# mLSTM scalings, decay and normalising moved to ScalarE; the last block's keys in a free operand's buffer; RWKV's first dense products issued beside that block

## The chip, the cores and the metric

The kernel runs on one core of one Trainium2 chip. The metric is the time of one execution on the device, in microseconds (us), as the median of several runs. The engines are named as in the profile: PE is TensorE's matrix multiply and PEld its weight load, DVE is VectorE, ACT is ScalarE, POOL is GpSimd, and SP is SyncE, whose queue issues all DMAs here.

## The reference, cut to what matters

One layer with four groups of heads (RWKV-7, pooling, mLSTM, retention) over 4096 tokens of 1024 channels: one input projection, four mixers of 256 channels each, one output projection with a gated embedding and a layer norm. The change concerns the mLSTM mixer and the first block of RWKV:

```
def mlstm_mix(qk, v, ig_pre, fg_pre, o_pre, conv_w, i_bias, f_bias, ln_w):
    qk = silu(causal_dwconv(qk, conv_w))          # 4 taps
    q, k = split(qk)
    ...
    d_log = where(causal, b[..., :, None] - b[..., None, :] + log_i[..., None, :], -inf)
    ...
    scores = einsum('bhcld,bhcsd->bhcls', q, k) * exp(d_log - m_t[..., None])
    num = einsum('bhcls,bhcsv->bhclv', scores, v) + s_inter * einsum('bhcvk,bhclk->bhclv', c_prev, q)
    den = sum(scores, -1) + s_inter * einsum('bhck,bhclk->bhcl', n_prev, q)
    h = num / maximum(abs(den), exp(-m_t))
    h = h * sigmoid(o_pre)
    h = head_norm(h) * ln_w

def rwkv7_mix(z, mu, ...):
    prev = pad(z)[:, :-1]
    z = z + (prev - z) * mu
    r, k, v, wl, al = split(z)
    ...
```

The mLSTM output is then multiplied by `silu(ml_g)`.

## The kernel before, in words

The tokens are worked in 16 blocks of 256 (`TB`), stage after stage: pooling, retention, mLSTM, RWKV (with the output gate's embedding), output. A dense product splits each operand into a rounded high part and a rest (`fetch`, L84 and L85: ACT casts, DVE or POOL subtracts) and adds three products into PSUM. The raw tiles of that split rotate through three buffers.

In `_mlstm`, `dense(b)` makes block b's projections: queries and keys as `zqk` (L145 to L147), and values, gates and output gates by seven products of Strassen's kind (`zoa` to `zod`, L1375 to L1377), whose operands lie in the weight pool and in the pool `mq`. `mix(b)` does the rest for the block: the convolution of queries and keys into `xc` (L1187 to L1194, tanh on ACT), then for each of two chunks of 128 tokens the decay `D` (a subtract and a maximum against the mask `big` on DVE, L1206; the exponential on ACT, L1209), scores `scm` (L1214), masked scores (L1216), `num` (L1219), the inter-chunk part `it` (L1222), the keys turned and scaled, `kt` and `kw` (L1227, L1229), the state update `dsm` and `Sm` (L1234, L1238), the sum `tot` (L1243, L1244) and the quotient (L1247 to L1251); then the gate, `head_norm` (L722 to L730; a power on POOL, L727), the weight `lnw` on POOL (L1255), the second gate (L1256) and the store. The loop calls `dense(i)` and `mix(i - 1)`, and a scheduler that follows its own estimates merges them into one fixed order on each engine. `xc` has one buffer (`XC`), `D` too (`DB`).

RWKV runs as a table of stages (`ORDER`), of which for block 0 the first are `la` (the low-rank columns), `k` and `r`: each is a dense product over eight pairs of input channels (`zla0`, 24 products; `z0k` and `z0r`, 48 each) and a mix with the token before (`mixed`, L264 to L268). The stage `l` takes `la` through the small matrices `LW` (loaded as `lraw`, split at L219 and L220), and `n` makes the key norms from squares `sq` on ACT (L366). `lraw`, a zeroed buffer that is written out to DRAM (L245 to L251) and `sq` share one buffer, in that order.

Of the kernel before, what the change touches and what calls it, by code (L numbers as in the profile page):

```python
# [42 lines left out]
class Trunk:  # L43
# [148 lines left out]
    def _rwkv_out(self, es):  # L192
# [16 lines left out]
        wg = [self.lazy("w_rw", i * G) for i in range(3)]  # L209
        wla = self.lazy("w_rw", 3 * G, P)  # L210
        wgate = self.lazy("w_rw", 3 * G + P)
        prm, omu = self.prm, self.omu
# [44 lines left out]
        def mixed(b, out, z, c0, n):  # L257

            zf, zl = bl[b]["zf"], bl[b]["zl"]
            with self.soon():  # L260
                A.copy(out=zl[:, c0:c0 + n], in_=z[:, :, TB - 1:TB].rearrange("p a o -> p (a o)"))
                for p in range(n):
                    c = c0 + p
                    A.mul(out=out[:, p], in_=z[:, p], mul=omu[:, c:c + 1])  # L264
                    V.scalar_tensor_tensor(out=out[:, p, 1:], in0=z[:, p, 0:TB - 1], scalar=prm[:, c:c + 1],
                                           in1=out[:, p, 1:], op0=ALU.mult, op1=ALU.add)
                first = out[:, :, 0:1].rearrange("p a o -> p (a o)")
                V.tensor_tensor(out=first, in0=first, in1=zf[:, c0:c0 + n], op=ALU.add)  # L268
# [25 lines left out]
        @stage  # L294
        def la(b):
            if b == 0:
                for w in (wla, wg[1], wg[0], wg[2]):
                    w()
            x = self.load_x(b)
            zf = self.zp.tile([P, 7], F32, name=f"zf{b}", tag="zf", bufs=2)  # L300
            zl = self.zp.tile([P, 7], F32, name=f"zl{b}", tag="zl", bufs=2)
            if b == 0:
                Q.memset(zf, 0.0)
            else:
                Q.tensor_tensor(out=zf, in0=bl[b - 1]["zl"], in1=prm[:, 0:7], op=ALU.mult)
            bl[b] = dict(zf=zf, zl=zl, x=x)
# [4 lines left out]
            la_ = self.zp.tile([P, 1, TB], F32, name=f"la{b}", tag="la", bufs=1)  # L311
            mixed(b, la_, z, 6, 1)
            la = la_[:, 0]
            with self.soon():
                A.activation(out=la[0:64], in_=la[0:64], func=AF.Tanh)
            bl[b]["la"] = la
# [1373 lines left out]
```

## Time and profile before

| | |
|---|---|
| median of 3 runs | 2850.34 us (2846.73 to 2855.72) |
| the profiled execution | 2850.36 us |
| its span, first to last instruction | 2848.6 us |
| PE / DVE / POOL / ACT busy | 95% / 80% / 40% / 34% |
| mean granted TensorE clock | 0.974 |
| mLSTM in the span | from about 656 us to 1260 us |

The profile is that of one execution. Busy shares are averages over stages with different limits; the granted clock is the share of TensorE's full 2.4 GHz that it was given, 0.50 being the lower of the two levels, 1.2 GHz. Idle time of an engine is shown with what ended it, and the chain of waits follows the work that ended last. Times in the traces are microseconds from the span's start.

### The profile page before, as it was taken

The numbers are of one execution on the slowest core, as the hardware profiler recorded it, in microseconds if no ns is written. First come the engines' busy times: TensorE is split into PE (matmuls) and PEld (weight loads), VectorE is DVE, ScalarE is ACT, GpSimd is POOL, SyncE is SP. The second block draws the span as 40 slices with busy tenths as digits, with TensorE's granted clock in tenths as the row PEclk, the third lists the DMA queues.
The fourth block names the chain that finished last, engine by engine and source line by source line (L and its number), as shares of the span: only waits on it lengthen the run. The fifth ranks groups of instructions, "written<-read, shape, count | busy, mean of one in ns | idle before, by whom it ended". The sixth has DMA issues, their size and how long they took to land.

```text
span 2848.6 us, 57425 instructions
## 1 busy us (share of the span) xinstructions
PE 2703.9 (95%) x21940; PEld 2422.4 (85%) x21940; DVE 2266.1 (80%) x5639; ACT 971.6 (34%) x2100; POOL 1142.9 (40%) x1263
## 2 busy tenths in 40 slices
PE   7799999998999999968999999999998999899997
PEld 7798888887999999958999999998887888777885
DVE  5767888887999999986888888888655666689997
ACT  3423232234433333323443434334322333432221
POOL 6555555554333333330232333224225111256665
PEclk9999999999999999969999999999999999999998
DMA  7753221223311111221111111113347444643441
GB/s 237 220 153 102 64 65 58 60 67 102 97 55 56 53 53 57 81 81 45 38 49 39 48 42 46 44 43 86 118 148 242 143 137 137 219 151 140 154 150 67
DMA packets 250500, 281.13 MB, mean 99 GB/s; under 512 B 69488, under 2 KB 166512, under 8 KB 250224
## 3 DMA queue, kind: packets, MB, share of 16 engines
q1 hardware_dynamic: 250224, 277.46, 31.0%
q8 instruction: 172, 2.82, 0.4%
q14 instruction: 104, 0.85, 0.1%
HBM read 209.69 MB, written 67.70 MB: 97 GB/s over the span
## 4 chain that ended last, share of the span: by engine, by line
PE 32%; DVE 14%; DMA 4%; POOL 3%; issue 3%; ACT 1%; SPq 0%; POOLq 0%; DVEq 0%; ACTq 0%
PE ry L273 3%; DVE ro L1582 2%; DVE ro L1561 1%; PE sa L273 1%; DVE ro L1564 1%; PE zg L154 1%; POOL ro L1565 1%; PE zg L155 1%; PE zg L156 1%; DVE so L1556 1%; PE zpe L145 1%; PE ds L273 1%; PE zpe L147 1%; DVE g L463 1%; PE zpe L146 1%
## 5 line engine op out<-in xcount | busy, mean ns | idle before, releaser
L1340 ACT CAST Ah<-xr 128x512 fp32r<-128x512 f32 x189 | 117.0, 620 | 277.9 <-PE zrb L1376 58.7
L1341 DVE TENSOR_TENSOR Al<-xr,Ah 128x512 fp32r<-128x512 f32 x135 | 98.1, 727 | 78.4 <-ACT Ah L1340 74.9
L681 POOL TENSOR_TENSOR SAV<-SAV,bon 64x256 f32<-64x256 f32 x64 | 42.2, 659 | 288.2 <-PE ry L273 282.4
L145 PE MATMUL zqk<-xh,wh_w_ml 128*128 128x256 f32 x512 | 148.8, 291 | 0.8 <-ACT xh L1082 0.8
L146 PE MATMUL zqk<-xl,wh_w_ml 128*128 128x256 f32 x512 | 149.0, 291 | 0.3 <-DVE xl L1083 0.3
L147 PE MATMUL zqk<-xh,wl_w_ml 128*128 128x256 f32 x512 | 149.1, 291 | 0.0
L85 DVE TENSOR_TENSOR xl<-rawx,xh 128x512 fp32r<-128x512 f32 x148 | 121.9, 826 | 29.4 <-ACT xh L84 28.5
L84 ACT CAST xh<-rawx 128x512 fp32r<-128x512 f32 x148 | 91.6, 619 | 138.3 <-DMA rawx<-in_xT 72.1
L1341 POOL TENSOR_TENSOR Al<-xr,Ah 128x512 fp32r<-128x512 f32 x54 | 71.3, 1321 | 132.2 <-ACT Ah L1340 71.7
L1565 POOL TENSOR_TENSOR ro<-ro,ln_b 128x512 f32<-128x512 f32 x64 | 100.7, 1592 | 53.8 <-DVE ro L1564 53.8
L870 POOL TENSOR_TENSOR rot<-rot,sw 128x256 f32<-128x256 f32 x64 | 69.3, 1084 | 93.8 <-DVE sw L869 89.6
L145 PEld LDWEIGHTS zqk<-xh,wh_w_ml 128*128 128x128 f32 x512 | 97.9, 191 | 2.9 <-ACT xh L1082 1.0
L147 PEld LDWEIGHTS zqk<-xh,wl_w_ml 128*128 128x128 f32 x512 | 98.0, 191 | 2.4
L146 PEld LDWEIGHTS zqk<-xl,wh_w_ml 128*128 128x128 f32 x512 | 98.0, 191 | 1.7 <-DVE xl L1083 0.5
L463 DVE SCALAR_TENSOR_TENSOR g<-gp,rc,c_rmask 128x128 f32<-128x128 f32 x256 | 71.1, 342 | 31.1 <-PE gp L273 31.1
L145 PE MATMUL zu<-xh,wh_w_pl 128*128 128x256 f32 x256 | 78.3, 306 | 15.0 <-ACT xh L84 8.5
L1360 POOL TENSOR_TENSOR xr<-xr,xr 128x512 f32<-128x512 f32 x27 | 35.2, 1303 | 141.1 <-DVE xr L1357 141.0
L146 PE MATMUL zu<-xl,wh_w_pl 128*128 128x256 f32 x256 | 77.4, 302 | 11.1 <-DVE xl L85 11.1
L664 DVE SCALAR_TENSOR_TENSOR S<-ds,eC,Se 64x64 f32<-64x64 f32 x256 | 72.4, 283 | 17.4 <-PE ds L273 12.4
L1189 DVE SCALAR_TENSOR_TENSOR xc<-zc,c_convw,xc 128x256 f32<-128x256 f32 x192 | 85.3, 492 | 0.4
L273 PE MATMUL ry<-SAV,g 64*64 64x64 f32 (+1 forms) x1024 | 84.0, 224 | 0.0
L802 DVE SCALAR_TENSOR_TENSOR dp<-s,c_pinv,us 64x256 f32<-64x256 f32 (+1 forms) x64 | 46.7, 729 | 44.4 <-POOL s L788 39.2
(1121 smaller groups left out, 10566.4 us busy)
## 6 DMA issues: line engine op xcount, KB each, us to landing
rawx<-in_xT SPq DMA_DIRECT2D x148, 256.0 KB, 3.3
xr<-in_xT SPq DMA_DIRECT2D x108, 256.0 KB, 2.9
mr<-in_xT SPq DMA_DIRECT2D x64, 256.0 KB, 3.0
rp<-in_x SPq DMA_DIRECT2D x64, 256.0 KB, 3.0
s<-rp SPq DMA_DIRECT2D x64, 256.0 KB, 2.6
yo<-y SPq DMA_DIRECT2D x16, 1024.0 KB, 4.9
ro<-s SPq DMA_DIRECT2D x16, 1024.0 KB, 5.0
out<-ro SPq DMA_DIRECT2D x32, 512.0 KB, 2.6
```

The source lines that it names most:

```text
L84: nc.scalar.copy(out=hi, in_=raw)
L85: eng.tensor_tensor(out=lo, in0=raw, in1=hi.bitcast(F32), op=ALU.subtract)
L145: nc.tensor.matmul(out, lh(k), rh(k), start=(k == 0 and (apart or i == 0)), stop=False, skip_group_check=True)
L146: nc.tensor.matmul(out, lh(k), rl(k), start=False, stop=False, skip_group_check=True)
L147: nc.tensor.matmul(out, ll(k), rh(k), start=False, stop=(k == nk - 1), skip_group_check=True)
L273: mm = lambda *args, **kw: keep(nc.tensor.matmul(*args, **kw))
L463: V.scalar_tensor_tensor(out=g1[cc][:, hh, p, e], in0=gp[hh][:, p, e], scalar=rc[:, cc, e, i:i + 1], in1=msk[:, 64 * e:64 * e + P], op0=AL ...
L664: V.scalar_tensor_tensor(out=Sn[hv, p, hv], in0=ds[hv, p], scalar=eC[hv, p, c:c + 1], in1=Se[hv, p], op0=ALU.mult, op1=ALU.add)
L1189: V.scalar_tensor_tensor(out=xc[:, t], in0=zc[t // 2][:, t % 2, j:j + TB], scalar=cw[:, t, j:j + 1], in1=xc[:, t], op0=ALU.mult, op1=ALU.add)
L1340: self.nc.scalar.copy(out=hi, in_=src)
L1341: eng.tensor_tensor(out=lo, in0=src, in1=hi.bitcast(F32), op=ALU.subtract)
L1565: Q.tensor_tensor(out=rg, in0=rg, in1=ln["ln_b", g], op=ALU.add)
```

## The change

In `mix`, multiplications by per-token or per-channel factors move from DVE to ACT as single instructions with a per-partition operand: the convolution's first tap, `kw` and `it`'s scaling (four pieces each per chunk), and the norm's subtract and scale (eight pieces, with `-mean*rs` as bias). The decay takes the mask by one maximum on DVE over all four heads, and the subtraction goes into ACT's exponential as its bias, in four pieces. The state's old part is scaled on POOL and added by two DVE steps. The quotient is made once for both chunks; its factor 0.5 goes into doubled constants (`VX`, `em`). `lnw` is multiplied into the gate `sg` on POOL, ahead of the chunks. The last block's `xc` takes a buffer of `mq` in place of the shared one. And behind the loop, still in mLSTM's pools and with its PSUM banks, `rwkv_first` issues RWKV's `la`, `k` and `r` products of block 0 with their mixes; `ORDER`'s three stages are passed over for that block.

```diff
@@ head_norm
+        if scaled:
+            nb = mv[:, :, 1]
+            nc.vector.scalar_tensor_tensor(out=nb, in0=mv[:, :, 0], scalar=-1.0, in1=rs, op0=ALU.mult, op1=ALU.mult)
+            for i in range(8):
+                nc.scalar.activation(out=y[:, i], in_=y[:, i], func=AF.Identity, scale=rs[:, i:i + 1], bias=nb[:, i:i + 1])
+            return
@@ mix
-            xc = p2.tile([P, 4, TB], F32, name=f"xc{b}", tag="xc", bufs=XC)
+            if b == self.NB - 1:
+                xc = mq.tile([P, 4, HW], F32, name=f"xc{b}", tag="q0")[:, :, 0:TB]
+            else:
+                xc = p2.tile([P, 4, TB], F32, name=f"xc{b}", tag="xc", bufs=XC)
             for t in (2, 0, 3, 1):
-                V.tensor_scalar(out=xc[:, t], in0=zc[t // 2][:, t % 2, 3:], scalar1=cw[:, t, 3:4], scalar2=None, op0=ALU.mult)
+                A.mul(out=xc[:, t], in_=zc[t // 2][:, t % 2, 3:], mul=cw[:, t, 3:4])
...
+            Q.tensor_tensor(out=sg, in0=sg, in1=lnw.unsqueeze(1).broadcast_to([P, 2, G]), op=ALU.mult)
...
+                V.tensor_tensor(out=Mb[c], in0=Mb[c], in1=big.unsqueeze(1).broadcast_to([P, 4, P]), op=ALU.max)
                 Dm = p2.tile([P, 2, 2, P], F32, name=f"D{b}_{c}", tag="D", bufs=DB)
-                for h in range(2):
-                    for p in range(2):
-                        i = 2 * p + h
-                        V.scalar_tensor_tensor(out=Dm[:, h, p], in0=Mb[c][:, i],
-                                               scalar=gt["u"][:, 4 * n + i:4 * n + i + 1], in1=big,
-                                               op0=ALU.subtract, op1=ALU.max)
-                A.activation(out=Dm, in_=Dm, func=AF.Exp, scale=-1.0)
+                for i in range(4):
+                    A.activation(out=Dm[:, i % 2, i // 2], in_=Mb[c][:, i], func=AF.Exp, scale=-1.0, bias=at("u", i))
...
-                V.tensor_tensor(out=kw, in0=kt.rearrange("p a (h v) -> p (a h) v", v=64),
-                                in1=gt["wk"][:, gc].unsqueeze(2).broadcast_to([P, 4, 64]), op=ALU.mult)
+                for i in range(4):
+                    A.mul(out=kw[:, i], in_=kt[:, i // 2, 64 * (i % 2):64 * (i % 2) + 64], mul=at("wk", i))
...
+                T = p1.tile([P, 2, 2, 65], F32, name=f"Td{b}_{c}", tag="tq")
+                Q.tensor_tensor(out=T.rearrange("p a h v -> p (a h) v"), in0=Sp.rearrange("p a h v -> p (a h) v"),
+                                in1=gt["sd"][:, 4 * n:4 * n + 4].unsqueeze(2).broadcast_to([P, 4, 65]), op=ALU.mult)
+                for h in range(2):
+                    hv = slice(64 * h, 64 * h + 64)
+                    V.tensor_tensor(out=Sn[hv, :, h], in0=T[hv, :, h], in1=ds[hv], op=ALU.add)
                 for i in range(4):
-                    V.scalar_tensor_tensor(out=Sn[hv, p, h], in0=Sp[hv, p, h],
-                                           scalar=gt["sd"][hv, 4 * n + i:4 * n + i + 1], in1=ds[hv, p],
-                                           op0=ALU.mult, op1=ALU.add)
+                    A.mul(out=tot[:, c, i], in_=it[:, i], mul=at("si", i))
+                V.tensor_tensor(out=tot[:, c], in0=tot[:, c], in1=num, op=ALU.add)
...
-            self.head_norm(p1, Y, HEAD_EPS, f"m{b}")
-            Q.tensor_tensor(out=Y, in0=Y, in1=lnw.unsqueeze(1).broadcast_to([P, 2, G]), op=ALU.mult)
+            self.head_norm(p1, Y, HEAD_EPS, f"m{b}", True)
@@ _mlstm, behind its loop
+        self.rwkv_first()
+    def rwkv_first(self):
...
+        for w in (self.wla, self.wg[1], self.wg[0], self.wg[2]):
+            w()
+        x = self.rw_begin(0)
+        z = self.bank("zla0", (P, 2, TB))
+        self.cols(z, self.wla(), x, 1)
+        self.rw_low(0, z)
+        for g, nm in ((1, "k"), (0, "r")):
+            z = self.bank(f"z0{nm}")
+            self.cols(z, self.wg[g](), x)
+            self.rw[0][nm] = self.zp.tile([P, 2, 15 + TB], F32, name=f"{nm}0", tag="z2")[:, :, 0:TB]
+            self.mixed(0, self.rw[0][nm], z, 2 * g, 2)
@@ ple's loop over ORDER
+                if i == 0 and nm in ("la", "k", "r"):
+                    continue
@@ constants
-        "big": np.where(causal, 0.0, 1.0e4).astype(f),
+        "big": np.where(causal, -3.0e38, 1.0e30).astype(f),
```

`rw_begin`, `rw_low` and `mixed` hold what stage `la` and its helper held before. The order that results, at three places; in a name the first number is the block, the next the chunk, and the last is a counter.

PE, from the last mLSTM chunk on, before:

```order
L1234 MATMUL dsm15_0_14148<-vx2_7369,kw15_0_14146 64x65 x4
L1222 MATMUL it15_1_14185<-Sm1_7366,xc15_14097 128x130 x2
L1227 MATMUL kt15_1_14188<-c_ident_192,xc15_14097 128x128 x2
L1219 MATMUL num15_1_14180<-vx3_7370,D15_1_14166 128x65 x4
L1234 MATMUL dsm15_1_14193<-vx3_7370,kw15_1_14191 64x65 x4
L154 MATMUL zla0_14420<-xh0_0_14394,wh_w_rw_768_14322 128x256
```

and now, a little after block 14's last `dsm`:

```order
L147 MATMUL zla0_14513<-xh0_2_14493,wl_w_rw_768_14414 128x256
L146 MATMUL z0k_14544<-xl0_2_14492,wh_w_rw_256_14433 128x256
L147 MATMUL z0k_14544<-xh0_2_14493,wl_w_rw_256_14432 128x256
L1194 MATMUL scm15_0_0_14294<-xc15_14262 128x128
L1194 MATMUL scm15_0_1_14295<-xc15_14262 128x128
L1202 MATMUL it15_0_14307<-Sm0_7365,xc15_14262 128x130
L1207 MATMUL kt15_0_14310<-c_ident_192,xc15_14262 128x128
L145 MATMUL zla0_14513<-xh0_4_14499,wh_w_rw_768_14415 128x256
```

All of RWKV's first products stood behind the last `dsm`; now they start behind block 14's last `dsm`, and block 15's chunks stand among them.

ACT, behind the last value copy, before:

```order
L1107 COPY vx3_7370<-mp115_13826 128x4x64
L84 CAST xh0_2_14400<-rawx0_2_14401 128x512
L84 CAST xh0_4_14406<-rawx0_4_14407 128x512
L84 CAST xh0_6_14412<-rawx0_6_14413 128x512
L84 CAST wh_w_rw_896_14643<-raww_rw_896_0_14644 128x512
L1209 ACTIVATE D15_0_14121<-D15_0_14121 128x512
```

and now:

```order
L1189 ACTIVATE D14_1_14171<-Mb29_14092,g_u_7727 128x128 x4
L1090 ACTIVATE so15_13954<-mu215_13982 128x256
L1090 ACTIVATE so15_13954<-mp515_13981 128x256
L1222 ACTIVATE tot14_14125<-it14_1_14189,g_si_7728 128x65 x4
L1210 ACTIVATE kw14_1_14195<-kt14_1_14192,g_wk_7729 128x64 x4
L84 CAST wh_w_rw_512_14469<-raww_rw_512_6_14482 128x512
L84 CAST xh0_0_14487<-rawx0_0_14488 128x512
L84 CAST xh0_2_14493<-rawx0_2_14494 128x512
L1189 ACTIVATE D15_0_14289<-Mb30_14252,g_u_7727 128x128 x4
```

Sixteen small pieces and four exponentials came in among the casts of weights and x.

ACT, at the low-rank matrices, before:

```order
L333 CAST lah0_14520<-la0_14445 64x256
L219 CAST LW0_14271<-lraw_14269 64x256
L219 CAST LW1_14272<-lraw_14269 64x256
L261 COPY zl0_14418<-z0k_14451 128x2
L264 ACTIVATE k0_14500<-z0k_14451,omu_206 128x256 x2
```

and now:

```order
L303 CAST lah0_14739<-la0_14538 64x256
L1294 ACTIVATE k0_14593<-z0k_14544,omu_206 128x256
L1291 COPY zl0_14511<-z0r_14600 128x2
L1294 ACTIVATE r0_14649<-z0r_14600,omu_206 128x256
L217 CAST LW0_14689<-lraw_14687 64x256
L217 CAST LW1_14690<-lraw_14687 64x256
```

`LW`'s casts now stand behind a copy that reads the finished `z0r`.

## Rows read from the trace of the kernel before

**Rows 1.** The page: busy time of each engine; 40 slices of PE and its clock.

```profile
PE 2703.9 (95%) x21940; PEld 2422.4 (85%) x21940; DVE 2266.1 (80%) x5639; ACT 971.6 (34%) x2100; POOL 1142.9 (40%) x1263
...
PE   7799999998999999968999999999998999899997
...
PEclk9999999999999999969999999999999999999998
```

**Rows 2.** Stretches: length, busy us (instructions) of each engine, PE clock, DMA share, GB/s.

```profile
740.00:1199.00 459.00, 455.83 (x3266) 432.35 (x3265) 434.01 (x1294) 168.38 (x387) 168.70 (x207) 1.00 0.19 58
1199.00:1275.00 76.00, 48.24 (x298) 43.69 (x297) 66.28 (x200) 25.04 (x54) 27.20 (x35) 0.69 0.32 97
```

**Rows 3.** Stretches of the seam between mLSTM and RWKV.

```profile
1212.40:1217.40 5.00, 0.00 (x0) 0.00 (x0) 4.96 (x8) 2.49 (x6) 3.54 (x4) 0.71 0.33 114
...
1222.70:1234.50 11.80, 0.01 (x1) 0.01 (x1) 11.69 (x29) 3.97 (x7) 2.53 (x2) 0.50 0.42 128
1234.50:1248.60 14.10, 12.15 (x60) 10.10 (x60) 12.59 (x50) 1.78 (x3) 4.38 (x3) 0.50 0.14 44
1248.60:1253.30 4.70, 4.70 (x30) 4.66 (x27) 4.42 (x16) 0.00 (x0) 0.00 (x0) 0.63 0.34 105
1253.30:1259.00 5.70, 5.70 (x50) 5.70 (x50) 4.62 (x22) 2.58 (x7) 3.20 (x2) 1.00 0.00 0
...
1268.90:1274.40 5.50, 5.38 (x35) 5.28 (x36) 3.98 (x12) 0.33 (x1) 0.89 (x2) 0.52 0.00 0
```

**Rows 4.** Timeline of PE: start, us, line, operation; idle before and its releaser.

```profile
1201.42 0.49 PE L1214 MATMUL scm<-xc 64*128 64x128 f32 x4 [1.08 <-DVE xc L1194]
...
1204.64 0.69 PE L1375 MATMUL zob<-mB,mB3whg 128*128 128x384 f32 x1 [1.87 <-DVE mu L1156]
...
1210.16 0.34 PE L1377 MATMUL zod<-mB,xl 128*128 128x384 f32 x1
...
1234.49 0.80 PE L1214 MATMUL scm<-xc 64*128 64x128 f32 x4 [11.86 <-DVE xc L1194]
...
1268.88 1.42 PE L273 MATMUL n<-ones,sq 128*64 128x2 f32 x16 [4.72 <-ACT sq L366]
```

**Rows 5.** Groups of DVE, 740 to 1199 us: busy, mean ns, idle before.

```profile
L1206 DVE SCALAR_TENSOR_TENSOR D<-Mb,g_u,c_big 128x128 f32<-128x128 f32 x109 | 41.2, 426 | 0.0
...
L1238 DVE SCALAR_TENSOR_TENSOR Sm<-Sm,g_sd,dsm 64x65 f32<-64x65 f32 x112 | 31.4, 280 | 1.4
...
L1256 DVE SCALAR_TENSOR_TENSOR Ym<-Ym,sgm 128x512 f32<-128x512 f32 x13 | 18.5, 1423 | 13.9 <-POOL Ym L1255 13.9
L1187 DVE TENSOR_SCALAR xc<-zc,c_convw 128x256 f32<-128x256 f32 x56 | 16.8, 361 | 0.0
L730 DVE TENSOR_TENSOR Ym<-Ym,rsm 128x512 f32<-128x512 f32 x13 | 16.1, 1235 | 4.9 <-POOL rsm L727 4.9
...
L1243 DVE TENSOR_TENSOR tot<-it,g_si 128x260 f32<-128x260 f32 x27 | 11.4, 421 | 1.3
```

**Rows 6.** Single lines of ACT: shortest, median and longest ns, first and last start.

```profile
L1012 ACT ACTIVATE ga_wk<-ga_u,ga_nm x1: 387/387/387, 707.8 to 707.8; 128x128 f32<-128x128 f32 x1
...
L1209 ACT ACTIVATE D<-D x32: 624/632/636, 721.6 to 1243.4; 128x512 f32<-128x512 f32 x32
```

**Rows 7.** Timeline of ACT: two with a per-partition operand in a row.

```profile
1262.50 0.83 ACT L345 ACTIVATE tw<-l,rhalf 128x256 f32<-128x256 f32 x2
```

**Rows 8.** The page's groups: DVE's split of an x tile.

```profile
L85 DVE TENSOR_TENSOR xl<-rawx,xh 128x512 fp32r<-128x512 f32 x148 | 121.9, 826 | 29.4 <-ACT xh L84 28.5
```

**Rows 9.** Timeline of SP's queue at RWKV's weights.

```profile
1195.86 14.06 SPq L83 DMA_DIRECT2D raww_rw<-in_w_rw  x9
```

**Rows 10.** Timeline of DVE: the split of `LW`.

```profile
1260.34 0.87 DVE L220 TENSOR_TENSOR LW<-lraw,LW 64x256 fp32r<-64x256 f32 x2
```

**Rows 11.** The chain of waits behind it: start, us, what.

```profile
1265.66 2.51 DMA xd<-rzero
...
1268.32 0.91 ACT sq L366 x2
```

More of the change, by code (lines that the diff above doesn't have):

```diff
@@ L207, in _rwkv_out @@
         Q = nc.gpsimd
[L209 to L212, printed above, removed]
+        wg, wla, wgate = self.wg, self.wla, self.wgate
+        prm = self.prm
         lraw = p1.tile([P, 2, P], F32, name="lraw", tag="km")
@@ L252, in _rwkv_out @@
         state = {"n": 0}
-        bl = {}
+        bl = self.rw
         t4 = lambda t: t.rearrange("p a (c t) -> p a c t", t=64)
         c5 = lambda t: t.rearrange("p a (c e) t -> p a c e t", e=2)
[L257 to L268, printed above, removed]
         st = {}
@@ L289, in group @@
                 self.zp.tile([P, 2, 15 + TB], F32, name=f"{nm}{b}", tag="z2")[:, :, 0:TB]
-            mixed(b, t, z, 2 * g, 2)
+            self.mixed(b, t, z, 2 * g, 2)
             bl[b][nm] = t
@@ L295, in la @@
         def la(b):
[L296 to L306, printed above, removed]
+            x = self.rw_begin(b)
             z = self.bank(f"zla{b}", (P, 1, TB))
@@ L310, in la @@
             yield from pieces([(z[:, 0], (f(w[0]), f(w[1])), x)], 3)
[L311 to L316, printed above, removed]
+            self.rw_low(b, z)
             yield 0.32
@@ L1243, in mix @@
-                V.tensor_tensor(out=tot, in0=it, in1=gt["si"][:, gc].unsqueeze(2).broadcast_to([P, 4, 65]), op=ALU.mult)
-                V.tensor_tensor(out=tot, in0=tot, in1=num, op=ALU.add)
-                den = p2.tile([P, 4], F32, name=f"den{b}_{c}", tag="den")
-                dn = tot[:, :, 64:65].rearrange("p h o -> p (h o)")
-                V.scalar_tensor_tensor(out=den, in0=dn, scalar=-1.0, in1=dn, op0=ALU.mult, op1=ALU.max)
-                V.tensor_tensor(out=den, in0=den, in1=gt["em"][:, gc], op=ALU.max)
@@ new lines, in mix @@
+            V.scalar_tensor_tensor(out=den, in0=dn, scalar=-1.0, in1=dn, op0=ALU.mult, op1=ALU.max)
+            V.tensor_tensor(out=den, in0=den, in1=gt["em"][:, 8 * b:8 * b + 8].rearrange("p (c h) -> p c h", c=2), op=ALU.max)
+            V.reciprocal(out=den, in_=den)
+            V.tensor_tensor(out=Y.rearrange("p c (h v) -> p (c h) v", v=64),
+                            in0=tot[:, :, :, 0:64].rearrange("p c h v -> p (c h) v"),
+                            in1=den.rearrange("p c h -> p (c h)").unsqueeze(2).broadcast_to([P, 8, 64]), op=ALU.mult)
@@ L1267, in _mlstm, with rw_begin, rw_low, mixed @@
             mix(i - 1)
+        self.rwkv_first()
+    def rwkv_first(self):
+        self.wg = [self.lazy("w_rw", i * G) for i in range(3)]
+        self.wla = self.lazy("w_rw", 3 * G, P)
+        self.wgate = self.lazy("w_rw", 3 * G + P)
+        self.rw = {}
+        for w in (self.wla, self.wg[1], self.wg[0], self.wg[2]):
[9 more added lines that the diff above has]
+            self.mixed(0, self.rw[0][nm], z, 2 * g, 2)
+    def rw_begin(self, b):
+        x = self.load_x(b)
+        zf = self.zp.tile([P, 7], F32, name=f"zf{b}", tag="zf", bufs=2)
+        zl = self.zp.tile([P, 7], F32, name=f"zl{b}", tag="zl", bufs=2)
+        if b == 0:
+            self.nc.gpsimd.memset(zf, 0.0)
+        else:
+            self.nc.gpsimd.tensor_tensor(out=zf, in0=self.rw[b - 1]["zl"], in1=self.prm[:, 0:7], op=ALU.mult)
+        self.rw[b] = dict(zf=zf, zl=zl, x=x)
+        return x
+    def rw_low(self, b, z):
+        la = self.zp.tile([P, 1, TB], F32, name=f"la{b}", tag="la", bufs=1)
+        self.mixed(b, la, z, 6, 1)
+        la = la[:, 0]
+        with self.soon():
+            self.nc.scalar.activation(out=la[0:64], in_=la[0:64], func=AF.Tanh)
+        self.rw[b]["la"] = la
+    def mixed(self, b, out, z, c0, n):
+        zf, zl = self.rw[b]["zf"], self.rw[b]["zl"]
+        V, A = self.nc.vector, self.nc.scalar
+        with self.soon():
+            A.copy(out=zl[:, c0:c0 + n], in_=z[:, 0:n, TB - 1:TB].rearrange("p a o -> p (a o)"))
+            for p in range(n):
+                c = c0 + p
+                A.mul(out=out[:, p], in_=z[:, p], mul=self.omu[:, c:c + 1])
+                V.scalar_tensor_tensor(out=out[:, p, 1:], in0=z[:, p, 0:TB - 1], scalar=self.prm[:, c:c + 1],
+                                       in1=out[:, p, 1:], op0=ALU.mult, op1=ALU.add)
+            first = out[:, :, 0:1].rearrange("p a o -> p (a o)")
+            V.tensor_tensor(out=first, in0=first, in1=zf[:, c0:c0 + n], op=ALU.add)
     RIGHT = {1: (0, 0), 2: (1, 0), 3: (1, 1), 0: (0, 1)}
```

18 lines of the change are left out of this document (7 added, 11 removed).

## The prediction

> **What bounds the kernel now.** First the page: the busy line, then the slices of TensorE (PE) and of its clock [rows 1]. The reader is to see that PE is busy 95% of the span, and that in the middle two slices stand out, the 18th (6 tenths busy, clock 6) and the 19th (8 tenths, clock 9). They are the seam between mLSTM and RWKV. Then the stretches [rows 2]: over fourteen steady mLSTM blocks PE is busy 455.83 of 459.00 us at full clock, and VectorE (DVE) 434.01; over the 76 us of the seam PE is busy 48.24 at a granted clock of 0.69. So the stage is PE's, with DVE close behind (31.0 us of work in a block of 32.8; ScalarE, ACT, has 12.0), and the seam is not PE's.
>
> Then the seam piece by piece [rows 3]: PE does nothing for 5.00 and again for 11.80 us while DVE is full, has 12.15 busy us of 14.10 at half clock, and reaches full clock only when RWKV's dense products stream, first at 0.63, then at 1.00. PE's waits [rows 4] say who holds it: block 15's dense work for DVE (1.08 and 1.87 us), the last mix for its keys (11.86, on DVE's convolution), and RWKV's norm `n` for ACT (4.72). The code gives the reason: block 15's keys share one buffer with block 14's, their convolution is DVE's, and RWKV's products stand behind all of it in PE's order.
>
> **The change part by part.** Below, Z is the end of block 15's last dense product, 1210.5 in the trace [rows 4].
>
> *DVE's relief in the steady blocks.* DVE loses in each block, gross, eight mask-and-subtract steps of 0.426, eight state updates of 0.280, four convolution starts of 0.361, two scalings of 0.421, and most of a 1.235 and a 1.423 that POOL had slowed [rows 5]. That is 10.6 us; two maxima, four adds and the smaller rest come instead, and I take 7 to 9 net. PE idles there only 3.2 us in 459 [rows 2], so the worth is bounded by that at the top; I take 2 us, some of it from before that stretch. Below, it is bounded by what ACT's longer queue can cost (a rival).
>
> *ACT's load.* With a per-partition operand, one of 128x128 alone takes 0.39 [rows 6], and two of 128x256 in a row 0.83, 0.42 each [rows 7]. In a row I take 0.30 for 128 columns and 0.25 for 64 (ends 0.20, if the time goes by columns, and 0.35, if hardly). Per block: eight exponentials at 0.30 for two of 0.632, four convolution starts at 0.42, and 24 pieces of 64 or 65 columns at 0.25: 1.1 + 1.7 + 6.0 = 8.8 us, 11 at the upper price. ACT goes from 12.0 to about 21 of 32.8 us, all beside PE. The sum stays under the period, so nothing is charged. POOL gets two state scalings of 128x260 per block, at most 2 us more on its 12.0 [rows 2], also beside PE. ScalarE's moved products are dearer than DVE's: four pieces at 0.25 replace one of 0.42. The Trainium skill, ScalarE: Activation LUTs, section Rules for kernel authors, says to keep plain multiplications on VectorE; by it the time would be that of the second rival.
>
> *The end of block 15's dense work.* DVE's backlog caused 1.08 + 1.87 us of waits, and PE came out of the second slowly: the first product behind it lasts 0.69, the last of the block 0.34 [rows 4]. With DVE ahead, and block 15's keys in the buffer of an operand that its second product frees, the waits go, 2.95 us, and I add 1 for the slow products: Z comes 4 us sooner (bounds 0, if DVE stays behind, and 5).
>
> *From Z to the end of `n`, in trace order of the new queues.* Before, this took 1270.3 - 1210.5 = 59.8 us (`n` starts at 1268.88 and lasts 1.42 [rows 4]). Now:
> - ACT, behind block 14's second chunk: a gate and a value copy, four exponentials (1.2), two gates (0.8), eight scalings (2.0), and hand-overs: PE can place that chunk's last product `dsm` at Z+7. Three casts of 0.62 and one DVE split of 0.83 [rows 6, 8] follow, or run beside it, and the first `zla0` starts at Z+8.
> - Weights and x pass through three raw buffers; nine tiles were issued in 14.06 us [rows 9], so one tile per 1.56, and a buffer comes round in 4.7. In SP's queue block 13's store and a mask load stand ahead of x, and wait for DVE and ACT until about Z+5. The last two x tiles follow one round behind the weight cast at Z+7: they are split at Z+14. By then the first 31 products (3.5 us at full, 7 at half clock) are done, so PE waits little for them.
> - ACT then has three casts of the gate's weights, each one buffer round away, to Z+17.5, and only behind them chunk 0's eight scalings (2.0), a cast, the low-rank mix, eight norm pieces (2.4), four exponentials (1.2): Z+27. Chunk 1's scalings (2.0), four casts (1.7), a k and an r copy: `LW`'s casts at Z+33, split on DVE at Z+35.
> - Behind `LW` stands a buffer that is zeroed and sent out before `n`'s squares can use it: 7.1 us in the trace (1261.21 to 1268.32 [rows 10, 11]), then squares 0.91, `n` 1.42: Z+44.
>
> PE's own work in that stretch is 120 dense products (14 us at full clock by the 50 in 5.70 us, 27 at half [rows 3]) and block 15's mix (12.15 busy at half clock, some 6 at full): 20 to 39 us from Z+8, in time for `LW` at Z+35 unless the clock stays down. So 59.8 becomes 44, a gain of 15.8; the ends are 36 (ACT never held by a raw tile) and 57 (half clock throughout).
>
> *Behind `n`.* The r products that followed `n` to the end of its stretch, at clock 0.52 [rows 3], are gone from there, 4 us; but the wait for `n` leaves PE idle as before, and the gate's products start at half clock in their place, so I count 2. What follows, the inverse of RWKV's first block and PE's next waits, moves with it and is charged at nothing.
>
> Sum: 2 + 4 + 15.8 + 2 = 23.8 us. The profiled execution took 2850.36, against a span of 2848.6, and stands on the median of the runs, 2850.34. That gives **2826 us**.
>
> **The rivals.**
> - *The clock stays down.* It stands at 0.50 through two stretches in which PE idles or works in pieces, and comes back only under an unbroken stream [rows 3]. If the new mixture of dense and small products does not lift it, PE needs 39 us from Z+8, the low-rank product comes at Z+47 and `n` ends at Z+57: 13 us of the 15.8 are lost, 2839. For it: `scm15` and its followers cut the stream. Against it: they are few between runs of nine or more products. The Trainium skill, TensorE: Matmul & The Clock Gate, section Part 1, says that the throttled state is the default and that activity releases it; by that rule the denser stream would recover, and the trace's return at 1253 agrees.
> - *ACT becomes what PE waits for, and the kernel is slower.* Place: between a chunk 0's `num` and chunk 1's. There is one buffer for the decays, so chunk 1's four exponentials (1.2 us) and DVE's two products (0.84, at the price of a scaling [rows 5]) wait for the first `num`; PE has 22 dense products, 2.5 us, and about 1 of small ones to cover 2.0. With ACT in order, the four key scalings or two casts in front use up the 1.5 left. Over 15 blocks it decides from 1.6 us of waiting a block, which eats the 23.8; at 2.4 us a block it is 36 lost, 2862. Against it: ACT is idle a third of each block and the key scalings are queued well ahead of that point.
> - *The overlap does not happen.* If x or the weights arrive only when the mix is done, RWKV's products run where they ran and only DVE's relief is left: 1.5 blocks of mix lie behind Z, 7 us of DVE work each, so about 10 us: 2840. For it: x passes SP behind the mask load. Against it: the earlier keys remove the 11.86 us wait in any case.
> - *Better than forecast*: `n` at Z+36 and all of the 3.2 us and more in the steady blocks: 2815 or less.
>
> **How the numbers follow.** Forecast 0.62, clock down 0.13, slower through ACT 0.08, no overlap 0.10, better 0.07. 0.3% is 8.6 us, about what a measurement of this kernel can tell from no change. Faster by more than that: the forecast, the clock case, half of the no-overlap case and the better one, 0.87. Within it: the other half, and a mild form of ACT's case (0.02): 0.07. Slower: 0.06. The range takes in the ends of the unknown prices and the clock case: 2814 to 2841; outside are ACT's case and parts of the other two.
>
> **What would show it.** Right: PE's idle stretches of 5 and 12 us gone, `zla0` starting near Z+8 between 1213 and 1219, r mixed before `n`, `n` near 1249, mLSTM blocks still 32 to 33 us apart. Wrong: PE waiting on ACT at `num` or `dsm` in every block; a clock of 0.50 through `zla0` to `z0r`; `zla0` behind the last mix; or the seam gained and lost again before RWKV's first chain step, which would mean that block 0's inverse, and not the dense work, set its start.

## The result and the profile after

The changed kernel takes 2817.54 us (median of 4 runs, 2816.85 to 2821.36), the kernel before beside it 2851.98 (2846.73 to 2855.72): a ratio of 0.9881, 95% interval 0.9868 to 0.9894. That is 34.4 us faster; forecast were 24, and the time lies in the range. The profiled execution took 2818.06, its span is 2816.3.

The page of the changed kernel, its busy line and the slices of PE and of its clock:

```profile
PE 2683.2 (95%) x21940; PEld 2408.3 (86%) x21940; DVE 2166.8 (77%) x5239; ACT 1104.5 (39%) x2644; POOL 1160.2 (41%) x1295
...
PE   8899999998999999988999999999998999999997
...
PEclk9899999999999999989999999999999999999998
```

The two weak slices of [rows 1], the 18th and the 19th, were 6 and 8 tenths busy and are now 8 and 8; the clock in the 18th is 8, where it was 6. The stretches that answer to [rows 2], and the seam in steps of ten:

```profile
740.00:1180.00 440.00, 440.00 (x3264) 423.37 (x3263) 348.05 (x952) 279.04 (x847) 182.09 (x236) 1.00 0.19 59
1199.00:1275.00 76.00, 62.61 (x493) 59.03 (x491) 52.41 (x164) 41.84 (x120) 17.66 (x35) 0.84 0.33 95
...
1199.00:1210.00 11.00, 5.61 (x32) 4.65 (x31) 7.75 (x20) 9.32 (x29) 3.93 (x4) 0.69 0.49 144
1210.00:1220.00 10.00, 10.00 (x71) 9.49 (x70) 8.28 (x28) 4.75 (x14) 3.55 (x3) 0.82 0.53 159
1220.00:1230.00 10.00, 10.00 (x87) 9.43 (x87) 4.93 (x12) 9.03 (x32) 3.27 (x11) 1.00 0.38 120
1230.00:1240.00 10.00, 3.98 (x29) 3.41 (x28) 8.91 (x39) 4.48 (x12) 1.60 (x7) 0.70 0.44 116
1240.00:1250.00 10.00, 8.53 (x58) 8.43 (x59) 7.19 (x19) 4.42 (x12) 4.97 (x9) 0.62 0.08 26
```

In the steady blocks DVE now works 348 of 440 us, ACT 279, and PE is shown busy all of the time, as it nearly was before. Over the seam PE is busy without a break from 1210 to 1230, at full clock in the second half of that, and then stops twice: 2.70 us for `LW` and 4.76 before `n`, with the clock at 0.70 and 0.62. The PE timeline's rows that answer to [rows 4], with RWKV's first products and `z1v`, the first product of block 1's values, which ends the seam:

```profile
1189.42 0.49 PE L1194 MATMUL scm<-xc 64*128 64x128 f32 x4 [1.03 <-DVE xc L1176]
1191.77 0.44 PE L1406 MATMUL zob<-mB,mB3whg 128*128 128x384 f32 x1 [1.32 <-DVE mu L1135]
1203.12 1.87 PE L1199 MATMUL num<-vx,D 128*128 128x65 f32 x8 [2.97 <-DVE D L1196]
1206.34 0.58 PE L145 MATMUL zla<-xh,wh_w_rw 128*128 128x256 f32 x1 [0.71 <-ACT xh L84]
...
1234.60 0.80 PE L258 MATMUL l<-lah,LW 128*128 128x256 f32 x2 [2.70 <-DVE LW L218]
...
1241.44 1.42 PE L258 MATMUL n<-ones,sq 128*64 128x2 f32 x16 [4.76 <-ACT sq L336]
...
1284.20 0.28 PE L154 MATMUL z1v<-xh,wh_w_rw 128*128 128x256 f32 x1
```

ACT's timeline gives the prices of the moved pieces (L705 the norm, L1189 the decay, L1222 and L1210 the scalings of `it` and `kt`):

```profile
1195.52 2.76 ACT L705 ACTIVATE Ym<-Ym,mvm,rsm 128x64 f32<-128x64 f32 x8 [1.76 <-DVE mvm L703]
...
1200.64 1.28 ACT L1189 ACTIVATE D<-Mb,g_u 128x128 f32<-128x128 f32 x4
...
1202.43 0.91 ACT L1222 ACTIVATE tot<-it,g_si 128x65 f32<-128x65 f32 x4
1203.22 0.92 ACT L1210 ACTIVATE kw<-kt,g_wk 128x64 f32<-128x64 f32 x4
```

So a piece of 64 columns costs 0.23 us with one per-partition operand and 0.35 with two, and one of 128 columns 0.32 (0.25 and 0.30 forecast).

Two measures compare the kernels. A block's **period** is the mean distance of ACT's copy of `zoa` over ten middle blocks (its third copy to its thirteenth). The **seam** runs from the last of these copies, in block 15, to `z1v`.

| | before | after |
|---|---|---|
| copy of `zoa`, block 1 and block 15 | 717.62, 1192.82 | 723.75, 1181.19 |
| period, middle ten | 33.83 | 32.53 |
| the first two blocks together | 69.6 | 65.4 |
| seam | 121.5 | 103.0 |

The fourteen intervals from block 1 to block 15 give 475.2 - 457.4 = 17.8 us, the seam 18.5. mLSTM's start takes 3.8 back (first `zqk` to the first copy, 61.3 before, 65.2 now). What stands ahead of mLSTM is 2.3 us longer in the second trace and what stands behind `z1v` 2.2 shorter, so these two cancel.

### The profile page after: what moved, and what is told of

The parts are those of the page before. It is cut to its first block, busy times and chain, and to the rows that moved or that the text cites. A ratio compares the mean times of both kernels' runs of the same rounds, so it can differ in the third digit from the quotient of the medians.

```text
span 2816.3 us, 57672 instructions
## 1 busy us (share of the span) xinstructions
PE 2683.2 (95%) x21940; PEld 2408.3 (86%) x21940; DVE 2166.8 (77%) x5239; ACT 1104.5 (39%) x2644; POOL 1160.2 (41%) x1295
## 3 DMA queue, kind: packets, MB, share of 16 engines
q1 hardware_dynamic: 250224, 277.46, 31.4%
## 4 chain that ended last, share of the span: by engine, by line
PE 65%; DVE 15%; DMA 5%; POOL 4%; issue 4%; ACT 2%; SPq 0%; POOLq 0%; DVEq 0%; ACTq 0%
PE ry L258 3%; PE zqk L145 2%; PE zqk L147 2%; PE zqk L146 2%; DVE ro L1613 2%; DVE ro L1592 1%; PE sa L258 1%; PE zg L154 1%; DVE ro L1595 1%; PE zra L1406 1%; PE zg L156 1%; PE zg L155 1%; POOL ro L1596 1%; PE zrb L1407 1%; PE zrc L1406 1%
## 5 line engine op out<-in xcount | busy, mean ns | idle before, releaser
L849 POOL TENSOR_TENSOR rot<-rot,sw 128x256 f32<-128x256 f32 x64 | 69.4, 1084 | 93.9 <-DVE sw L848 89.1
L145 PEld LDWEIGHTS zqk<-xh,wh_w_ml 128*128 128x128 f32 x512 | 97.9, 191 | 2.5 <-ACT xh L1061 1.0
L634 DVE SCALAR_TENSOR_TENSOR S<-ds,eC,Se 64x64 f32<-64x64 f32 x256 | 72.4, 283 | 19.1 <-PE ds L258 14.4
L659 POOL TENSOR_TENSOR Y<-Y,SAV 64x256 f32<-64x256 f32 x64 | 50.2, 784 | 75.7 <-DVE Y L655 65.8
```

The lines of the kernel that those rows point to most:

```text
L145: nc.tensor.matmul(out, lh(k), rh(k), start=(k == 0 and (apart or i == 0)), stop=False, skip_group_check=True)
L634: V.scalar_tensor_tensor(out=Sn[hv, p, hv], in0=ds[hv, p], scalar=eC[hv, p, c:c + 1], in1=Se[hv, p], op0=ALU.mult, op1=ALU.add)
```

## The experiments

Each ratio is to the kernel before, measured in the same session. Period, first two blocks, seam and DVE are read from the one execution that was profiled; DVE is its busy time per block in the ten blocks of the period.

| run | ratio (95%) | period | first two | seam | DVE |
|---|---|---|---|---|---|
| before | 1 | 33.83 | 69.6 | 121.5 | 31.8 |
| after | 0.9881 (0.9868 to 0.9894) | 32.53 | 65.4 | 103.0 | 25.3 |
| e1 moves to ACT alone | 0.9921 (0.9904 to 0.9937) | 32.49 | 66.0 | 110.6 | 25.3 |
| e2 overlap and keys alone | 0.9987 (0.9978 to 0.9996) | 33.84 | 69.6 | 117.4 | 31.8 |
| e3 no overlap | 0.9887 (0.9868 to 0.9906) | 32.51 | 64.8 | 103.9 | 25.1 |
| e4 no keys' buffer | 0.9877 (0.9862 to 0.9891) | 32.49 | 65.4 | 104.9 | 25.1 |
| e5 DVE load ahead of `D` | 0.9945 (0.9926 to 0.9963) | 32.86 | 70.5 | 108.9 | 28.9 |
| e6 DVE load behind `Ym` | 1.0006 (0.9996 to 1.0015) | 34.03 | 67.6 | 123.2 | 31.4 |
| e7 before, less DVE work | 0.9966 (0.9953 to 0.9979) | 32.88 | 69.9 | 115.2 | 28.4 |
| e8 two `D` buffers | 0.9928 (0.9911 to 0.9945) | 32.68 | 69.4 | 103.5 | 26.4 |
| e9 gates and seam | 0.9872 (0.9856 to 0.9889) | 32.44 | 70.5 | 97.9 | 25.5 |
| e10 after, less DVE work | 0.9905 (0.9890 to 0.9920) | 32.66 | 68.9 | 101.1 | 23.2 |
| e11 decay alone | 0.9977 (0.9966 to 0.9988) | 33.16 | 72.8 | 116.9 | 30.4 |
| e12 seam alone | 0.9876 (0.9859 to 0.9893) | 32.51 | 65.4 | 103.0 | 25.3 |

### The parts apart: e1 to e4

e1 is the changed kernel without the two edits below; e3 is without the first alone, e4 without the second alone. e2 keeps both and takes `mix` and its constants from the kernel before.

```diff
-        self.rwkv_first()
-                if i == 0 and nm in ("la", "k", "r"):
-                    continue
@@ the second
-            if b == self.NB - 1:
-                xc = mq.tile([P, 4, HW], F32, name=f"xc{b}", tag="q0")[:, :, 0:TB]
```

> The moves to ScalarE alone: RWKV's first products go back behind the last mix, block 15's keys go back into the shared buffer. Theory A (the two parts add: the moves give the steady blocks' 12 to 15 us and 1.5 at the end of the dense work, the seam's some 17 us come from the overlap and the keys): about 2837 us, 14 to 16 below the kernel before, and the seam from the last zqk product to n as long as before within 4 us. Theory B (the moves also carry the seam, because block 15's mix is VectorE's work): about 2828, with the seam 8 to 10 us shorter.

> The overlap and the keys' buffer alone; every operation of the mix stays on VectorE as before. Theory A: about 2834 us (17 to 18 below the kernel before), with steady blocks 33.9 us apart as before. Theory B: VectorE still runs behind, so x and the splits of RWKV's operands come late and the overlap is worth at most 8: about 2845, blocks 33.9 us apart.

> The changed kernel with RWKV's first products back behind the last mix; the keys' own buffer stays. Theory A: the wait for the keys (11.86 us before) goes anyway, some of it is refound behind them, RWKV's products lose their cover: about 2829 us, 11 above the changed kernel. Theory B: the seam needs little beyond the relief and the keys: about 2823. The steady blocks stay 32.7 us apart under both.

> The changed kernel with block 15's keys back in the shared buffer; the overlap stays. Theory A: RWKV's products fill the wait for the keys, and ScalarE, not the keys, sets n: 2818 to 2821 us. Theory B: the keys set the order of the seam, the mix of block 15 ends some 5 to 10 us later and n with it: 2823 to 2828.

Theory A falls: e1, e2 and e3 come out on theory B's side, e3 even under it (2817.3 us). Only e4, at 2815.78, is nearer to A's 2818 to 2821. The moves alone bring 0.79% of the 1.19%, with the whole of the steady gain and 10.9 us of the seam's 18.5. (These 10.9 are from a profiled execution of 2818.58 us, 8.3 under e1's median, so the split of the seam is less sure than the ratio.) The overlap and the keys' buffer without them bring 0.13%: in e2 RWKV's first products start 28.7 us behind the copy in place of 55.8, but PE then waits 10.94 us for DVE's split of `LW`. And with the moves either of the two does for both: e3 and e4 cannot be told from the changed kernel. PE's timeline shows it, in e1, then e3, then e4 (block 15's copies of `zoa` are at 1177.66, 1174.13 and 1177.84):

```profile
1229.26 0.58 PE L154 MATMUL zla<-xh,wh_w_rw 128*128 128x256 f32 x1
...
1244.03 0.94 PE L261 MATMUL n<-ones,sq 128*64 128x2 f32 x16 [0.33 <-ACT sq L342]
...
1288.24 0.28 PE L154 MATMUL z1v<-xh,wh_w_rw 128*128 128x256 f32 x1
```

```profile
1220.65 0.58 PE L154 MATMUL zla<-xh,wh_w_rw 128*128 128x256 f32 x1
...
1235.47 0.94 PE L261 MATMUL n<-ones,sq 128*64 128x2 f32 x16
...
1278.00 0.28 PE L154 MATMUL z1v<-xh,wh_w_rw 128*128 128x256 f32 x1
```

```profile
1199.59 0.56 PE L145 MATMUL zla<-xh,wh_w_rw 128*128 128x256 f32 x1
...
1240.53 1.42 PE L258 MATMUL n<-ones,sq 128*64 128x2 f32 x16 [4.80 <-ACT sq L336]
...
1282.73 0.28 PE L154 MATMUL z1v<-xh,wh_w_rw 128*128 128x256 f32 x1
```

In e4 RWKV's first products start 24.8 us earlier against block 15 than in e3 (21.8 us behind the copy, 46.5 there), and `z1v` comes 1.0 us later. With the keys early, block 15's mix ends early and RWKV's products follow at once; with the products early, they fill the wait for the keys. Both buy the same idle time of PE, so the second adds nothing: in the seam PE is idle for 28.5 us before, 22.2 in e1, 15.0 in e3, 19.1 in e4 and 15.9 in the changed kernel.

### VectorE's load and the steady blocks: e5 to e7, e11

Theory W said that short waits for DVE are booked as PE's busy time, theory S that the order of dense and small products is what got cheaper.

e5 and e6 put idle steps back into the changed kernel (e6: twelve on `Y[:, i % 2, 0:P]`, ahead of the store):

```diff
+                for i in range(6):
+                    V.scalar_tensor_tensor(out=scr, in0=Mb[c][:, i % 4], scalar=gt["u"][:, 0:1], in1=big, op0=ALU.subtract, op1=ALU.max)
```

> The changed kernel with twelve idle 128x128 steps per block put back on VectorE, six behind each chunk's mask maximum and so in front of its product for D (12 x 0.43 = 5.1 us per block; VectorE from 26 to 31 of 32.7 us, as loaded as before the change). Theory W (the steady blocks were held by short waits of TensorE for VectorE that the profile books as busy): the block period goes back from 32.7 to 33.5 to 34.0 us, and num starts within 0.25 us of the end of D's product again in many chunks (22 of 54 before, 2 of 51 after); about 2832 to 2840 us with the seam's share. Theory S (the blocks are shorter because of the order in which small and dense products alternate): 32.6 to 32.9 us, the kernel at 2818 to 2824.

> The same twelve idle steps per block, but behind the block's last gate product, where nothing of TensorE's waits for them directly. Theory W in its narrow form (only VectorE work in front of D counts): period at most 33.0 us, 2818 to 2825 us. Theory W in its wide form (VectorE takes its work in order, so any load makes the next D late): 33.4 us or more, about 2830 us. Theory S: 32.6 to 32.9 us.

e7 leaves out the mean's subtraction in mLSTM's norm and one convolution tap:

```diff
-                for j in range(3):
+                for j in range(1, 3):
```

> The kernel before with two steps of VectorE left out in every mLSTM block and nothing moved to ScalarE: the norm's subtraction of the mean and the convolution's first of four taps (4 x 0.49 us and about 1 us, together some 2.9 us per block). Theory W: the period falls from 33.9 to 33.1 to 33.3 us, and the seam shortens by some 4: about 2835 us. Theory S: 33.9 us, and only the seam gains: about 2846.

> The kernel before with only the decay changed: the mask by one maximum on VectorE (0.81 us per chunk), the subtraction in ScalarE's exponentials, four per chunk. VectorE loses 8 x 0.43 - 2 x 0.81 = 1.8 us per block, right in front of D's product. Theory W: the period falls by 0.4 to 0.6 us to 33.3 to 33.5, 2838 to 2842 us. If only the sum of all moves helps (a threshold near VectorE's saturation): 33.8 to 33.9 us and 2844 to 2850.

DVE's load moves the kernel in both directions (in e5, e6 and e7 nothing else was edited). Taking work off DVE in the kernel before, with nothing given to ACT, shortens the period from 33.83 to 32.88 and the seam by 6.3 (e7); the decay alone, whose subtraction goes to ACT, brings 33.16 and 4.5 (e11). Both periods are lower than theory W had forecast. Load behind `Ym` undoes the whole change (e6): the next block's steps stand behind it in DVE's order. e5 was a half miss: twelve steps ahead of `D` cost 0.3 us a block and not 0.8 to 1.3, though they cost 5.9 in the seam and 5.1 in the first two blocks, and `num` starts within 0.25 us of the end of `D` in only 5 of 55 chunks. But the two loads were not the same: an idle step took 391 ns in e5 and 576 in e6 (means, 785 to 1110 us), so DVE has 28.9 us of work a block in e5, not the 31 that were meant, and 31.4 in e6. The windows of the ten blocks, before, after, e5 and e6 (DVE is the third engine):

```profile
787.20:1125.52 338.32, 336.44 (x2401) 318.09 (x2400) 317.90 (x949) 122.70 (x281) 123.41 (x150) 1.00 0.18 56
789.17:1114.51 325.34, 325.34 (x2399) 312.61 (x2398) 252.77 (x691) 204.23 (x620) 131.33 (x170) 1.00 0.18 58
791.63:1120.22 328.59, 326.63 (x2392) 311.52 (x2391) 288.89 (x821) 204.74 (x622) 136.38 (x170) 1.00 0.18 57
789.78:1130.03 340.25, 332.93 (x2396) 314.97 (x2396) 313.78 (x819) 208.50 (x621) 129.55 (x170) 1.00 0.17 55
```

Over all runs the period goes with what DVE has to do, wherever in the block it stands: 32.4 to 32.7 us up to a load of 26.4, 32.9 at 28.4 and 28.9, 33.2 at 30.4, 33.8 to 34.0 at 31.4 and 31.8. So e5 tells nothing of the place of the load. In e6 some of the waits are long enough to show in the groups of PE (740 to 1170 us; busy, mean ns, idle before):

```profile
L1200 PE MATMUL num<-vx,D 128*128 128x65 f32 x200 | 28.8, 269 | 2.6 <-DVE D L1197 2.6
...
L1203 PE MATMUL it<-Sm,xc 128*128 128x130 f32 x100 | 17.8, 298 | 5.1 <-DVE Sm L1221 5.1
```

To see where the hidden part lies, the starts of PE's products were read one by one over the ten middle blocks, and the time to the next start put down to the product that began it (us per block):

| | before | e11 | e7 | after | e6 |
|---|---|---|---|---|---|
| `zqk` | 12.70 | 12.31 | 12.19 | 12.23 | 12.81 |
| `zoa` to `zod` | 14.89 | 14.84 | 14.93 | 14.76 | 14.76 |
| `scm` | 2.37 | 2.12 | 2.00 | 1.76 | 2.04 |
| `kt` | 0.43 | 0.43 | 0.40 | 0.28 | 0.70 |
| `num`, `it`, `dsm` | 3.42 | 3.46 | 3.34 | 3.50 | 3.70 |

Of the 1.30 us per block between before and after, 0.47 is `zqk`, 0.61 `scm`, 0.15 `kt`, 0.13 the `zo` products; the rest goes 0.08 the other way. Most of the `zqk` part, 0.30, is theory W's: in seven of the ten blocks a `num` starts 0.5 to 0.7 us after a `zqk` product where 0.12 is usual, and 0.05 us after DVE's `D` ends. PE's timeline before shows one:

```profile
1005.24 0.28 PE L146 MATMUL zqk<-xl,wh_w_ml 128*128 128x256 f32 x1
1005.76 0.88 PE L1219 MATMUL num<-vx,D 128*128 128x65 f32 x6 [0.24 <-DVE D L1216]
```

From start to start this is 0.52, 0.40 more than usual, but the modelled end of the product ahead hides 0.16 of that: only 0.24 is shown as idle. Over the ten blocks these waits are 0.19 us per block shown as idle and 0.11 hidden. The `scm` part is theory S's. In the same timeline before, and then after:

```profile
1002.60 0.71 PE L1214 MATMUL scm<-xc 64*128 64x128 f32 x4
```

```profile
1026.95 0.72 PE L1194 MATMUL scm<-xc 64*128 64x128 f32 x8
```

Eight instructions in the time of four. One by one, the eight start in pairs under 0.02 us apart, and the four 0.21 and 0.11 apart. In PE's order of before, a chunk's scores for one half of the heads often stand apart from those for the other half (a product of DVE for `D`, which needs one whole half, starts at 903.65, between four `scm` at 900.96 and four at 904.93); after, more of them alternate by halves, and these start together: in pairs under 0.02 us apart, 58 in ten blocks against 20. No wait stands in the `scm` part: none of its starts is over 0.25 us from the next. So both theories hold, S for more of it than W. e6 shows W by itself: its `scm` is 0.33 cheaper than before, yet its period is 0.2 longer, since in nine of the ten blocks an `it` starts 0.7 to 1.5 us after a `zqk` product, waiting for DVE's `Sm`. W also acts through S: DVE's product for `D` frees each half's score bank, and when less is asked of DVE, the planner places both halves side by side; e7 and e11, with lighter DVE work, got part of the cheaper `scm` too. That link was argued from the order, not tested: the planner gave PE another order in every one of these runs, and none held the order and changed the load.

### What is left: e8, e9, e10, e12

e8 gives `D` a second buffer (`DB = 2`) and `Ym` one in place of two.

> The changed kernel with two buffers for the decays D (room made by one buffer in place of two for Ym). If D's one buffer holds TensorE (ScalarE's exponentials of chunk 1 wait for the first num, the mechanism of the rival in which ScalarE is waited for): the period falls to 32.2 or less and the wait of 2.97 us at block 14's second num goes: about 2808. If VectorE's load was what held the blocks, and it is gone: 32.6 to 32.8 us, 2814 to 2818.

The period is the second theory's (32.68), so `D`'s buffer is not what holds PE. The time is neither's: 2825.84 us, with 4.0 us more in the first two blocks and the seam unchanged. The wait of 2.97 us at block 14's second `num` did go, but others came in the seam (2.74 at `zob`, 1.63 at `dsm`, 6.23 before `n`). Whether `Ym`'s single buffer or the new order cost that stays open.

e10 is e7's omitted tap, in the changed kernel.

> The changed kernel with the convolution's first of four taps left out, 4 x 0.49 us of VectorE per block less. If hidden waits for VectorE still stretch the blocks: the period falls in the same measure as when VectorE's load fell before (0.7 us for some 2.9), by 0.4 to 0.5 to 32.2 us, about 2809. If they are used up (num starts 2.26 us behind D in the median, and 25.5 us of dense and 6.8 of small products leave little): 32.5 to 32.7 us, 2812 to 2817.

The period does not fall (32.66, with DVE at 23.2 us a block), so DVE's load is used up as a means. The ratio is 0.9905 in place of 0.9881, with intervals that just overlap; the first two blocks take 3.5 us more in its trace and the seam 1.9 less.

e9 and e12 aim at ACT's queue at mLSTM's start and before `n`. e12 is e9 without its first edit:

```diff
-        gt, md = self.gates(cp, es)
+        with self.soon():
+            gt, md = self.gates(cp, es)
@@ _rwkv_out, around LW's load, casts and splits
+        with self.soon():
@@ zeros sent out from a state tile, not from the buffer shared with lraw and sq
-        zero = p1.tile([P, 512], F32, name="rzero", tag="km")
...
-                nc.sync.dma_start(out=XD[i][:, e].rearrange("j a c -> j (a c)"), in_=zero[0:64])
+                for g in range(2):
+                    nc.sync.dma_start(out=XD[i][:, e, 4 * g:4 * g + 4].rearrange("j a c -> j (a c)"),
+                                      in_=S0[i][0:64].rearrange("p a v -> p (a v)"))
```

> The changed kernel, with three edits aimed at what its trace still shows: the gates' copies at mLSTM's start ahead of ScalarE's weight casts, LW's casts ahead of the last r copy, and the zeroed buffer gone (zeros are sent out from a state tile), so that n's squares stand before l's tanh. Theory R (what remains is queue order on ScalarE): mLSTM's block 1 starts 2 to 3 us earlier against the first zqk (59.7 us in the changed kernel, 57.0 before), n follows l within 2 us in place of 6.8, z1v comes 3 to 5 us earlier against block 15: ratio 0.985 to 0.987, some 5 us below the changed kernel. Theory Q (VectorE's chain through tw sets z1v, not n): the start's 2 to 3 us alone, ratio 0.987 to 0.989.

> The changed kernel with the seam's edit of the last but three runs alone: LW's load given priority, the zeroed buffer gone, so n's squares stand before l's tanh; the gates as in the changed kernel. In the run with the gates' edit too, z1v came 97.9 us behind block 15's first za copy (103.0 in the changed kernel), but the first two mLSTM blocks took 70.5 us (65.4). Theory R: z1v at 97 to 99 us, first blocks at 65 to 66, period 32.5: ratio 0.9855 to 0.987, 4 to 5 us below the changed kernel. Theory Q (it was the gates' edit): z1v at 102 to 103 and no change against the changed kernel, 0.988.

In e12 the wait before `n` falls from 4.76 to 0.53, and `n` comes 3.3 us earlier against block 15; `z1v` does not move (103.0). PE's timeline shows where 2.2 of the 3.3 us go, after first and then e12:

```profile
1253.44 1.37 PE L258 MATMUL gp<-AR,BK 64*128 64x128 f32 x16
```

```profile
1249.54 0.46 PE L259 MATMUL gp<-AR,BK 64*128 64x128 f32 x2 [1.24 <-DVE AR L382]
1250.91 1.16 PE L259 MATMUL gp<-AR,BK 64*128 64x128 f32 x14 [0.92 <-DVE ST L414]
```

DVE's timeline tells why, after first and then e12 (`AR` is the first operand of block 0's chain that comes late):

```profile
1247.01 0.76 DVE L375 TENSOR_TENSOR BK<-ta,tw 128x256 f32<-128x256 f32 x2
1247.69 1.59 DVE L378 SCALAR_TENSOR_TENSOR AR<-k,c_prm,E 128x128 f32<-128x128 f32 x2
```

```profile
1242.99 1.22 DVE L376 TENSOR_TENSOR BK<-ta,tw 128x256 f32<-128x256 f32 x2
1245.89 0.69 DVE L1236 SCALAR_TENSOR_TENSOR Ym<-Ym,sgm 128x512 f32<-128x512 f32 x1 [1.67 <-ACT Ym L706]
1246.50 0.68 DVE L174 SCALAR_TENSOR_TENSOR sg<-sg,zg 128x512 f32<-128x512 f32 x1
1247.84 0.69 DVE L85 TENSOR_TENSOR xl<-rawx,xh 128x512 fp32r<-128x512 f32 x1 [0.67 <-ACT xh L84]
1248.45 0.61 DVE L379 SCALAR_TENSOR_TENSOR AR<-k,c_prm,E 128x128 f32<-128x128 f32 x2
```

Against block 15's copy, `BK` is done 2.5 us earlier (66.6 after, 64.1 in e12), and `AR` starts 1.8 us later (66.5, 68.3): block 15's last gate (held by ACT's eight norm pieces), the gate's product and an x split now stand ahead of it. The 4.76 us before `n`, PE's longest wait in the seam, was no bound by itself: when it shrank, others came behind it. e9's seam is 5 us shorter (its order has all of `AR` ahead of the split, and `AR` starts at 64.1); its first two blocks give 5 us back. Neither e9 nor e12 can be told from the changed kernel, so no run beat it by more than the measurement is uncertain.

## Why the prediction was right, and where it was wrong

The direction and range held, the sum was 10 us short, and the shares were wrong. By its steps:

- **DVE's relief in the steady blocks, 2 us: this step failed.** It measured 17.8, less 3.8 at mLSTM's start. "The worth is bounded by that at the top" was the error: PE's 3.2 us of shown idle [rows 2] is no bound. Of the 1.30 us per block, 0.19 was shown as idle and 0.11 was waiting hidden under modelled ends of products; most of the rest was a dear order of small products, which counts as busy. DVE lost 6.5 us a block (31.8 to 25.3), a little less than the 7 to 9 taken. The "block of 32.8" is 459 us over fourteen; the copies of `zoa` stand 33.83 apart, so the stretch holds 13.6 blocks, and "still 32 to 33 us apart" describes the kernel after and not the one before.
- **End of block 15's dense work, 4 us:** from its copy of `zoa` to Z, 17.7 became 15.3, so 2.4. The waits for `xc` and `mu` shrank to 1.03 and 1.32 and did not go.
- **From Z to the end of `n`, 15.8 us:** 59.8 became 1242.86 - 1196.45 = 46.4, so 13.4. The steps stood where they were put (`zla0` at Z+9.9 against 8, `LW` split at Z+39 against 35, `n` done at Z+46.4 against 44), each about two to four late, 2.97 of it by `D` of block 14's second chunk. But the reason given was half wrong: e1 has 10.9 us of the seam without overlap or keys, and e3 nearly all of it (17.6 of 18.5) without overlap.
- **Behind `n`, 2 us:** from the end of `n` to `z1v`, 44.0 became 41.3, so 2.7. But "moves with it" does not hold: in e12 an earlier `n` alone brings `z1v` no sooner, since DVE's chain behind it came later.
- **mLSTM's start** was left out: ACT's gate copies stand behind its weight casts, and PE waits 1.33, 0.70 and 1.00 us for them (0.74 in all before). Of the 3.8 us, 2.7 are lost ahead of the first `zoa` product of block 1; with the copies put ahead of the casts (e9) 2.3 of these 2.7 come back.

That the time lies in the range is in part luck: the relief brought 12.0 us more than its step, the three steps of the seam 3.3 less than theirs, and the case that was to be better than forecast was priced with `n` at Z+36, which did not come. Of the signs, PE's stretches of 5 and 12 us are gone, r is mixed before `n`, and no steady block waits for ACT; `zla0` and `n` came at 1206.34 and 1241.44, ahead of the times named, since block 15 itself came 11.6 us sooner.

The rivals: the clock came back under the stream, 0.82 in 1210 to 1220 and 1.00 in 1220 to 1230, and was lower again with the waits for `LW` and `n`, 0.70 and 0.62 in the next two stretches. The Trainium skill, TensorE: Matmul & The Clock Gate, section Part 1, calls the throttled state the default, which activity releases; the trace agrees. ACT did not become a wait of the steady blocks: PE shows none there. "The overlap does not happen" was rightly priced at 10 us in the seam for the relief alone, but not for the relief with early keys, where the overlap is worth nothing measurable (e3). The Trainium skill, ScalarE: Activation LUTs, section Rules for kernel authors, says to keep plain multiplications on VectorE. The trace agrees on the price, 0.92 us for four pieces on ACT against 0.42 for one step on DVE, and not on the outcome: e1, with the moves, is 0.79% faster, and ACT had the idle time that DVE had not.

## What to carry to other kernels

A matrix engine that is shown 99% busy can still be slowed by its helpers: before bounding a gain by its idle time, read its products from start to start, and look for waits under modelled ends and, here the larger part, for small products that could start together. When a load is put back as a test, measure what it came to before comparing its places (e5, e6). Take load off the fullest helper first; two edits that buy the same idle time count once, so price each without the other. A long wait on one engine bounds nothing if the work behind it is held by another queue.

## What was not expected

Score products of 64 rows that alternate between the halves of the heads start under 0.02 us apart, while two of the same half start 0.11 to 0.21 apart; between before and after this makes 0.61 us of a 33.83 us block. And the first two mLSTM blocks took between 64.8 and 72.8 us in kernels that differ by a few steps, as much as most of the edits are worth; their order was not studied further.
